# A hybrid attention and convolution block on one core: raw compressed values computed in channel layout

## The chip, the cores and the metric

The kernel runs on one NeuronCore of one Trainium2 chip. The metric is device time in microseconds (us) of one execution. TensorE (PE) multiplies, VectorE (DVE) and ScalarE (ACT) work on tiles and read and write PSUM, GpSimd (POOL) works on SBUF tiles, and the SP queue issues most DMAs. PEld is the weight load of TensorE, which runs beside its matmuls.

## The reference

One decoder block on x of shape (1, 512, 1024), float32:

- h = rms_norm(x), then one wide product h @ w_in, which is split into queries, three pairs of keys and values (compressed, selected, window; 4 groups of 64 channels each), attention gates, two convolution inputs and two merge gates.
- Compressed keys and values: `compress_blocks` cuts the 512 tokens of a group into blocks of 32 with a stride of 16, adds a position embedding, flattens a block to 32 x 64 numbers, and runs `silu(blocks @ w1) @ w2`. Keys are rotated (rope) ahead of it, values are not.
- Attention: 16 heads in 4 groups, three softmax branches (compressed, selected, window), summed with gates.
- A causal convolution of 31 taps over 1024 channels, layer norm over the channels, silu, and a product with w_conv_out; merged with the attention by two gates, multiplied by w_out and added to x.
- A SwiGLU feed-forward part with 2816 hidden channels, and a final rms_norm.

## The kernel before

Every float32 product is made of three matmuls with operands split into a high and a low part (`mm3`, lines 211 to 213). A weight piece is loaded raw by SP (`wr`, line 120), rounded by ACT to its high part (`wh`, line 136), and POOL (DVE in some stages) subtracts to get the low part (`wl`, line 137).

A product with w_in comes in two layouts. **Token layout** (`tok_g`): the activations hT are the stationary operand, 256 columns of weights move, and a PSUM tile `ptk` holds 2 x 128 tokens by 256 channels; 256 output channels take 96 matmuls of 256 columns. **Channel layout** (`chan_g`): a weight block is the stationary operand, all 512 tokens move, and a PSUM tile `pch` holds 128 channels by 512 tokens; 256 output channels take 48 matmuls of 512 columns. Both take their two PSUM tiles from the pool `dense`, two buffers.

The work around the change stands in this program order: convolution inputs (`ub_g`, `ua_g`), then `cmp_raw(C_KC, True)` for raw compressed keys, `cmp_raw(C_VC, False)` for raw compressed values, `keys(C_KS, 0)`, `cmp_prep` and `keys(C_KW, 1)`, then `cmp_mlp` for the compressed keys beside the selected values, and so on up to the first queries. `cmp_raw` fills two chunk buffers `kcraw` of 128 x 512: rows 0 to 63 hold the even tokens of two groups, rows 64 to 127 the odd ones. Its inner function `evT` (line 449) makes each buffer with four ACT copies of 64 x 256 from a PSUM tile that holds channels by tokens. In `cmp_raw` for values the token layout is used, ACT copies each `ptk` to SBUF (`kd`, line 458), and TensorE transposes it back to channels by tokens in eight 128 x 128 transposes (`tv`, line 466).

`cmp_prep` later adds the positions on DVE (`kctmp`, line 488), rounds on ACT (`kchi`, line 491) and subtracts on DVE (`kclo`, line 492). `cmp_mlp` multiplies them (`phid`). The convolution's 31 taps per channel block are DVE instructions on a PSUM accumulator (`cacc`, line 794) that lie between all of this.

Attention runs as 32 units (4 groups, 2 head pairs, 4 query blocks). A unit makes its scores in PSUM tiles `sc` (lines 700 to 703, pool of two buffers), DVE takes the maxima (`nm`, line 705), ACT the exponentials (`P`, line 708), DVE makes the factors `R` (lines 715 and 718), ACT scales P with them (line 723), TensorE transposes P (`tP`, line 732), ACT and DVE split that (`pth`, `ptl`, lines 735 and 736), and TensorE multiplies with the values (`pv`, lines 756 to 760), from where ACT copies to `pvt` (line 763). Products with w_in and w_conv_out in small steps are put between these (`fill`). The layer norm of the convolution is done in five stages between units 16 and 21: among them `pstat` and `pvar` (matmuls on lines 811 and 826), eight subtractions of the mean on DVE (line 815), eight multiplications on DVE (line 833), and eight Silu on ACT (line 835), which need another activation table than the exponentials.

The order on each engine is not the program order. The framework's scheduler lists the instructions by its own estimate of when each may run, and each engine then runs its list in order. An edit early in the program can therefore move instructions far behind it.

Of the kernel before, what the change touches and what calls it, by code (L numbers as in the profile page):

```python
# [10 lines left out]
F32 = mybir.dt.float32  # L11
# [11 lines left out]
NT = S // 128  # L23
# [13 lines left out]
def hybrid_block(  # L37
# [8 lines left out]
    nc = tc.nc  # L46
# [15 lines left out]
    pa = astack.enter_context(tc.tile_pool(name="att", bufs=1))  # L62

    def acts(name, dt=F32):
        return ap.tile([128, S], dt, name=name, tag="A")
# [16 lines left out]
    def trp(name):  # L82
        return ps.tile([128, 512], F32, name=name, tag="tr", bufs=2)


    idn = cp.tile([128, 128], F32, name="idn")
# [80 lines left out]
    hT_hi = [acts(f"hThi{k}", F32R) for k in range(KT)]  # L167
    hT_lo = [acts(f"hTlo{k}", F32R) for k in range(KT)]
# [15 lines left out]
    for th in range(2):  # L184
# [6 lines left out]
        for k in range(KT):  # L191
            p = trp("hT")
            for j in range(2):
                nc.tensor.transpose(p[:, j * 128:(j + 1) * 128], hs[2 * th + j][:, k * 128:(k + 1) * 128], idn)
            ev = nc.scalar.activation(hT_hi[k][:, hsl], p[:, :256], AF.Copy, scale=g_mix[:, k:k + 1])  # L195
# [19 lines left out]
    def chan_g(src, c0, act_hi, act_lo, evac, ncol=256, halves=((0, S),), ws=None):  # L215

        nm_ = (ncol + 127) // 128
        given, ws = ws, ws or []

        def part(p, m, kh, kk, n0=0, n1=S):  # L220
            wh, wl = ws[kh][kk]
            w = min(128, ncol - 128 * m)
            sl = slice(128 * m, 128 * m + w)
            k = 4 * kh + kk
            mm3(p[:w, n0:n1], wh[:, sl], wl[:, sl], act_hi[k][:, n0:n1], act_lo[k][:, n0:n1],
                k == 0, k == KT - 1)

        fine = phase["fine"]
        if fine:
            ws.append(wload(src, 0, 4, c0, ncol))  # L230
            yield 0
        p = [dense("pch") for _ in range(nm_)]
        for n0, n1 in halves:
            for kh in range(2):
                if not fine and not given and n0 == 0:
                    ws.append(wload(src, 4 * kh, 4, c0, ncol))
                for m in range(nm_):
                    if fine and m == 0 and kh == 0:
                        ws.append(wload(src, 4, 4, c0, ncol))
                    for kk in range(4):  # L240
                        part(p[m], m, kh, kk, n0, n1)
                        if fine and kk < 3:
                            yield 640
                    if kh and n1 == S:
                        evac(m, p[m])
                    if fine:
                        yield 640
                if not fine:
                    yield 0

    def tok_g(src, c0, act_hi, act_lo, evac, tts=(0, 1, 2, 3)):

        nu = len(tts) // 2
        ws = []

        def part(p, u, kh, j, kk):
            wh, wl = ws[kh][kk]
            t = tts[2 * u + j]
            sl = slice(128 * t, 128 * t + 128)
            k = 4 * kh + kk  # L260
            mm3(p[:, 256 * j:256 * j + 256], act_hi[k][:, sl], act_lo[k][:, sl], wh, wl,
                k == 0 and j == 0, k == KT - 1)

        fine = phase["fine"]
        if fine:
            ws.append(wload(src, 0, 4, c0, 256))
            yield 0
        p = [dense("ptk") for _ in range(nu)]
        for kh in range(2):
            if not fine:  # L270
                ws.append(wload(src, 4 * kh, 4, c0, 256))
            elif kh == 0:
                ws.append(wload(src, 4, 4, c0, 256))
            for u in range(nu):
                for j in range(2):
                    for kk in range(4):
                        part(p[u], u, kh, j, kk)
                        if fine and kk % 2 and (kk, j) != (3, 1):
                            yield 640
                if kh:  # L280
                    evac(tts[2 * u], p[u].rearrange("p (j c) -> p j c", j=2))
                if fine:
                    yield 640
            if not fine:
                yield 0

    def chan(*a, **k):
        for _ in chan_g(*a, **k):
            pass

    def tok(*a, **k):
        for _ in tok_g(*a, **k):
            pass
# [26 lines left out]
    for bits in (7, 15, 24, None):  # L320
        if bits is None:
            part = rest
        else:
            q = 2.0 ** (bits - 3)
# [44 lines left out]
    def run_all(*gens):  # L369
        gens = list(gens)  # L370
        while gens:
            for g_ in list(gens):
                if next(g_, gens) is gens:
                    gens.remove(g_)
# [44 lines left out]
    def roped_tokens(c0, evT):  # L419

        tiles = []

        def ev(u, p):
            kd = pa.tile([128, 2, 4, 64], F32, name="kd", tag="pt", bufs=5)
            nc.scalar.copy(kd[:, :, :, 16:64], p.rearrange("p j (h d) -> p j h d", d=64)[:, :, :, 16:64])

            def dst(A, B):
                nc.vector.tensor_add(kd[:, :, :, 0:16], A, B)

            rope_rows(p, u, 4, dst)  # L430
            tiles.append(kd)

        yield from tok_g(w_in, c0, hT_hi, hT_lo, ev)
        for gp in range(2):
            q = trp("tk")
            for t in range(NT):
                src = tiles[t // 2][:, t % 2, 2 * gp:2 * gp + 2, :].rearrange("p g d -> p (g d)")
                nc.tensor.transpose(q[:, 128 * t:128 * t + 128], src, idn)
            evT(gp, q)


    def cmp_raw(c0, roped):
        raw = [pa.tile([128, S], F32, name="kcraw", tag="q", bufs=8) for _ in range(2)]

        def evT(gp, q):
            for gg in range(2):
                v = q[64 * gg:64 * gg + 64, :].rearrange("p (u a) -> p a u", a=2)
                for a in range(2):
                    nc.scalar.copy(raw[gp][64 * a:64 * a + 64, 256 * gg:256 * gg + 256], v[:, a, :])

        if roped:
            run_all(roped_tokens(c0, evT))
            return raw
        tiles = []

        def ev(u, p):
            kd = pa.tile([128, 2, 4, 64], F32, name="kd", tag="pt", bufs=5)
            nc.scalar.copy(kd.rearrange("p j h d -> p j (h d)"), p)
            tiles.append(kd)

        tok(w_in, c0, hT_hi, hT_lo, ev)
        for gp in range(2):
            q = trp("tv")
            for t in range(NT):
                src = tiles[t // 2][:, t % 2, 2 * gp:2 * gp + 2, :].rearrange("p g d -> p (g d)")
                nc.tensor.transpose(q[:, 128 * t:128 * t + 128], src, idn)
            evT(gp, q)
        return raw

    def cmp_prep(raw, pos, w2):  # L470
# [167 lines left out]
    def query_split(qd, pr):  # L638
# [11 lines left out]
        return res  # L650

    raw_k = cmp_raw(C_KC, True)
    raw_v = cmp_raw(C_VC, False)
    vals = []
    run_all(keys(C_KS, 0))
# [298 lines left out]
    for n in range(32):  # L954
        g, pr, i = n // 8, n // 4 % 2, n % 4
# [166 lines left out]
    for t in range(NT):  # L1122
        sl = slice(128 * t, 128 * t + 128)

        for c in ((0, 256), (256, 512)) if t == NT - 1 else ((0, 512),):
# [3 lines left out]
            j = 1 + c[0] // 256  # L1129
# [40 lines left out]
```

## Time and profile before

| | us |
|---|---|
| median of three runs | 975.17 (974.79 to 975.36) |
| the profiled execution's own time | 974.84 |
| its span, first to last instruction | 973.1 |
| TensorE busy in the span | 940.4 |
| VectorE, ScalarE, GpSimd busy | 633.1, 545.1, 234.9 |

The span is cut by stage as follows: norm and convolution inputs up to about 85 us, keys, values and compression up to about 200 us, attention with the convolution's end up to about 530 us, w_out and the feed-forward part to the end. In lines of the timeline the columns are start, duration, engine, line, operation, output <- inputs, tile shape, count, and in square brackets the idle time of the engine before and what ended it. Matmul durations in them overlap; what one costs in a stream is the distance between starts.

### The profile page before, as it was taken

To read this page: it belongs to the slowest core of one execution; us is meant where nothing else is said; L and a number is where in the kernel's file an instruction comes from. 1 tells how busy PE (TensorE), PEld (TensorE's weight loads), DVE (VectorE), ACT (ScalarE), POOL (GpSimd) and SP (SyncE) were. 2 spreads that over 40 slices of the span, in tenths; PEclk is the share of its full clock that TensorE was granted. 3 is DMA by queue.
4 is the path that set the end of the run, shared out by engine and by line. 5 is a ranking of instruction groups with operands and counts; after the bars stand their busy time and mean duration, and the time that the engine had idled before them with its cause. 6 is when DMAs were issued, how large, how long until landed. Compare 5 with 4: busy or idle time off the path is not lost.

```text
span 973.1 us, 14959 instructions
## 1 busy us (share of the span) xinstructions
PE 940.4 (97%) x5306; PEld 797.5 (82%) x5306; DVE 633.1 (65%) x1254; ACT 545.1 (56%) x1273; POOL 234.9 (24%) x256
## 2 busy tenths in 40 slices
PE   5999989899999999989999999999999999999996
PEld 5889979888888977877778878988888888888886
DVE  6799999987999987676876877633333343322512
ACT  6533545558879887999984776533333333322412
POOL 3545447853353342622322000000000000000000
PEclk9999989999999999999999999999999999999999
DMA  7333324542121111111212166633333323322302
GB/s 225 90 106 88 87 72 121 134 109 55 45 66 44 34 45 44 44 33 55 98 56 76 59 201 188 180 96 100 91 105 88 107 87 108 97 96 95 118 29 87
DMA packets 77599, 89.03 MB, mean 91 GB/s; under 512 B 5896, under 2 KB 65620, under 8 KB 77524
## 3 DMA queue, kind: packets, MB, share of 16 engines
q1 hardware_dynamic: 76676, 87.38, 30.0%
q8 instruction: 42, 0.69, 0.3%
q0 software_dynamic: 144, 0.52, 0.2%
q14 instruction: 33, 0.27, 0.1%
q10 hardware_dynamic: 704, 0.17, 0.1%
HBM read 85.96 MB, written 2.10 MB: 90 GB/s over the span
## 4 chain that ended last, share of the span: by engine, by line
PE 85%; DVE 7%; ACT 4%; issue 1%; DMA 1%; POOL 1%; SPq 0%; POOLq 0%; ACTq 0%; DVEq 0%
PE pf L211 8%; PE pf L212 8%; PE pf L213 8%; PE pch L213 7%; PE pch L211 7%; PE pch L212 7%; PE ptk L211 4%; PE ptk L212 4%; PE ptk L213 4%; PE pd L211 4%; PE pd L213 4%; PE pd L212 4%; PE tP L732 3%; PE sc L700 2%; PE sc L701 2%; PE pv L756 2%
## 5 line engine op out<-in xcount | busy, mean ns | idle before, releaser
L137 POOL TENSOR_TENSOR wl<-wr,wh 128x512 fp32r<-128x512 f32 x128 | 167.2, 1318 | 229.8 <-ACT wh L136 179.5
L136 ACT CAST wh<-wr 128x512 fp32r<-128x512 f32 x228 | 140.1, 622 | 145.0 <-PE pf L212 52.6
L794 DVE SCALAR_TENSOR_TENSOR cacc<-z,cw,cacc 128x512 f32<-128x512 f32 x232 | 165.5, 748 | 3.8 <-ACT cacc L792 1.7
L211 PE MATMUL pf<-h2hi,wh 128*128 128x512 f32 (+1 forms) x384 | 142.3, 372 | 0.6 <-ACT h2hi L1034 0.6
L212 PE MATMUL pf<-h2lo,wh 128*128 128x512 f32 (+1 forms) x384 | 142.5, 372 | 0.0
L213 PE MATMUL pf<-h2hi,wl 128*128 128x512 f32 (+1 forms) x384 | 142.4, 372 | 0.0
L137 DVE TENSOR_TENSOR wl<-wr,wh 128x512 fp32r<-128x512 f32 x100 | 68.7, 689 | 109.6 <-ACT wh L136 108.1
L213 PE MATMUL pch<-hThi,wl 128*128 128x512 f32 (+1 forms) x272 | 107.3, 395 | 1.5 <-POOL wl L137 1.5
L211 PE MATMUL pch<-hThi,wh 128*128 128x512 f32 (+1 forms) x272 | 107.3, 396 | 1.2 <-ACT hThi L195 1.2
L212 PE MATMUL pch<-hTlo,wh 128*128 128x512 f32 (+1 forms) x272 | 107.5, 396 | 0.0
L149 DVE TENSOR_TENSOR wl<-wr,wh 128x512 fp32r<-128x512 f32 x76 | 51.6, 689 | 61.9 <-ACT wh L148 61.8
L148 ACT CAST wh<-wr 128x512 fp32r<-128x512 f32 (+1 forms) x84 | 50.1, 604 | 73.7 <-PE pd L213 50.9
L708 ACT ACTIVATE P<-sc,nm 128x32 f32<-128x32 f32 (+3 forms) x192 | 84.7, 446 | 11.2 <-DVE nm L705 9.2
L1136 POOL TENSOR_TENSOR rstd<-rstd,half 128x1 f32<-128x1 f32 x4 | 2.2, 547 | 359.6 <-DVE rstd L1135 359.6
L211 PEld LDWEIGHTS pf<-h2hi,wh 128*128 128x128 f32 x384 | 72.0, 188 | 13.2 <-ACT h2hi L1034 0.8
L211 PE MATMUL ptk<-wh,hThi 128*128 128x256 f32 x288 | 82.7, 287 | 0.0
L213 PEld LDWEIGHTS pf<-h2hi,wl 128*128 128x128 f32 x384 | 72.2, 188 | 12.6
L212 PEld LDWEIGHTS pf<-h2lo,wh 128*128 128x128 f32 x384 | 72.2, 188 | 12.4
L212 PE MATMUL ptk<-wl,hThi 128*128 128x256 f32 x288 | 81.2, 282 | 0.0
L213 PE MATMUL ptk<-wh,hTlo 128*128 128x256 f32 x288 | 81.0, 281 | 0.0
L705 DVE TENSOR_REDUCE nm<-sc 128x1 f32<-128x32 f32 (+3 forms) x192 | 68.8, 381 | 16.8 <-PE sc L703 15.5
L211 PE MATMUL pd<-wh,ahi 128*128 128x512 f32 (+1 forms) x184 | 70.0, 380 | 0.8 <-DVE x L1092 0.8
(234 smaller groups left out, 2133.0 us busy)
## 6 DMA issues: line engine op xcount, KB each, us to landing
wr<-in_w_in_dram SPq DMA_DIRECT2D x100, 256.0 KB, 2.8
wr<-in_w_ffn_gate_dram SPq DMA_DIRECT2D x48, 256.0 KB, 2.7
wr<-in_w_ffn_up_dram SPq DMA_DIRECT2D x48, 256.0 KB, 2.7
wr<-in_w_ffn_down_dram SPq DMA_DIRECT2D x44, 256.0 KB, 2.5
wr<-in_w_out_dram SPq DMA_DIRECT2D x32, 256.0 KB, 2.6
x<-in_x_dram SPq DMA_DIRECT2D x8, 512.0 KB, 5.0
wr<-in_w_conv_out_dram SPq DMA_DIRECT2D x16, 256.0 KB, 2.7
wr<-in_cmp_k_w_dram SPq DMA_DIRECT2D x8, 256.0 KB, 2.6
```

The lines of the kernel that those rows point to most:

```text
L136: nc.scalar.copy(hi[:, sl, :ncol], raw[:, sl, :ncol])
L137: eng.tensor_sub(lo[:, sl, :ncol], raw[:, sl, :ncol], hi[:, sl, :ncol].bitcast(F32))
L148: nc.scalar.copy(hi, raw)
L149: (nc.vector if phase["lo_dve"] else nc.gpsimd).tensor_sub(lo, raw, hi.bitcast(F32))
L211: nc.tensor.matmul(o, lh, rh, start=first, stop=False, skip_group_check=True)
L212: nc.tensor.matmul(o, lh, rl, start=False, stop=False, skip_group_check=True)
L213: nc.tensor.matmul(o, ll, rh, start=False, stop=last, skip_group_check=True)
L700: nc.tensor.matmul(sc[:, :e - a], qh[:, tsl], K[:, a:e], start=True, stop=False)
L705: nc.vector.tensor_reduce(out=nm[:, b:b + 1], in_=sc[:, ba - a:be - a], axis=AX.X, op=OP.max, negate=True)
L708: nc.scalar.activation(P[:, ba:be], sc[:, ba - a:be - a], AF.Exp, bias=nm[:, b:b + 1], accum_out=Dn[:, b, hh:hh + 1])
L732: nc.tensor.transpose(t4[:, 256 * b + 128 * hh:256 * b + 128 * hh + 128], Ps[hh][:, key_blk(j, b)], idn)
L794: nc.vector.scalar_tensor_tensor(cts[c] if j == TAPS - 1 else a, z[:, j:j + S], cw[:, j, c:c + 1], a, op0=OP.mult, op1=OP.add)
```

## The change

In `cmp_raw` the raw values are now made with the channel layout, and `evT` copies each finished PSUM tile straight into its chunk buffer. The SBUF tiles `kd` of the values, their two ACT copies and the eight transposes are gone. All lines below move up by 13.

```diff
@@ cmp_raw
         if roped:
             run_all(roped_tokens(c0, evT))
             return raw
-        tiles = []
-
-        def ev(u, p):
-            kd = pa.tile([128, 2, 4, 64], F32, name="kd", tag="pt", bufs=5)
-            nc.scalar.copy(kd.rearrange("p j h d -> p j (h d)"), p)
-            tiles.append(kd)
-
-        tok(w_in, c0, hT_hi, hT_lo, ev)
-        for gp in range(2):
-            q = trp("tv")
-            for t in range(NT):
-                src = tiles[t // 2][:, t % 2, 2 * gp:2 * gp + 2, :].rearrange("p g d -> p (g d)")
-                nc.tensor.transpose(q[:, 128 * t:128 * t + 128], src, idn)
-            evT(gp, q)
+        chan(w_in, c0, hT_hi, hT_lo, evT)
         return raw
```

The lists of the engines differ from there on. Three places follow, each before and after.

**ACT at the raw values.** Before, the copies of the transposed raw keys are followed by casts of weights (`wh`), the two copies to `kd`, and eight copies to the chunk buffers from `tv`:

```order
L449 COPY kcraw<-tk 64x256 x8
L136 CAST wh<-wr 128x512 x2
L458 COPY kd<-ptk 128x512
L136 CAST wh<-wr 128x512
L458 COPY kd<-ptk 128x512
L136 CAST wh<-wr 128x512
L449 COPY kcraw<-tv 64x256 x8
```

After:

```order
L449 COPY kcraw<-tk 64x256 x8
L136 CAST wh<-wr 128x512 x2
L449 COPY kcraw<-pch 64x256 x4
L136 CAST wh<-wr 128x512 x2
L449 COPY kcraw<-pch 64x256 x4
```

The two copies to `kd` are gone, and the eight chunk copies now come in two fours, one behind each `pch`.

**DVE at the preparation of the compressed keys** (`kst` is the low part of the selected keys, `kctmp` and `kclo` belong to the compressed ones). Before:

```order
L488 TENSOR_TENSOR kctmp<-kcraw,cpos 128x8x64
L566 TENSOR_TENSOR kst_837<-tk,kst_837 64x128
L488 TENSOR_TENSOR kctmp<-kcraw,cpos 128x8x64
L566 TENSOR_TENSOR kst_837<-tk,kst_837 64x128
L488 TENSOR_TENSOR kctmp<-kcraw,cpos 128x8x64 x2
L492 TENSOR_TENSOR kclo<-kctmp,kchi 128x8x128
L566 TENSOR_TENSOR kst_837<-tk,kst_837 64x128
L492 TENSOR_TENSOR kclo<-kctmp,kchi 128x8x128
```

After (line 488 is now 475, 566 is 553, 492 is 479):

```order
L475 TENSOR_TENSOR kctmp<-kcraw,cpos 128x8x64
L553 TENSOR_TENSOR kst_837<-tk,kst_837 64x128
L475 TENSOR_TENSOR kctmp<-kcraw,cpos 128x8x64 x2
L553 TENSOR_TENSOR kst_837<-tk,kst_837 64x128
L475 TENSOR_TENSOR kctmp<-kcraw,cpos 128x8x64
L553 TENSOR_TENSOR kst_837<-tk,kst_837 64x128
L479 TENSOR_TENSOR kclo<-kctmp,kchi 128x8x128 x2
```

Three subtractions for `kst` instead of two now stand between the first `kctmp` and the first `kclo`.

**ACT at the last stage of the convolution's norm**, beside units 21 and 22 of the attention. Before, from the copy `pvt` to the table load of the exponentials (`ct` are the convolution's channel blocks):

```order
L763 COPY pvt<-pv 64x256
L835 ACT_TABLE_LOAD
L835 ACTIVATE ct_2182<-ct_2182,vec 128x512
L723 ACTIVATE P<-P,R 128x256 x4
L835 ACTIVATE ct_2184<-ct_2184,vec 128x512
L835 ACTIVATE ct_2379<-ct_2379,vec 128x512
L835 ACTIVATE ct_2381<-ct_2381,vec 128x512
L835 ACTIVATE ct_2461<-ct_2461,vec 128x512
L835 ACTIVATE ct_2956<-ct_2956,vec 128x512
L835 ACTIVATE ct_3567<-ct_3567,vec 128x512
L835 ACTIVATE ct_4007<-ct_4007,vec 128x512
L708 ACT_TABLE_LOAD
```

After (723 is now 710, 835 is 822), the first five of these rows; seven more Silu and the table load of the exponentials follow:

```order
L750 COPY pvt<-pv 64x256
L136 CAST wh<-wr 128x512
L710 ACTIVATE P<-P,R 128x256 x4
L822 ACT_TABLE_LOAD
L822 ACTIVATE ct_2120<-ct_2120,vec 128x512
```

A cast and all four scalings of P now stand ahead of the table load, and all eight Silu behind it. On PE, between the product with the compressed values (`pv<-pc`) and the first score matmul of unit 22 that waits for these exponentials, there stand 33 `pch` matmuls of 512 columns and eight transposes before, 17 and eight after; the rows just ahead of that score matmul are, after:

```order
L211 MATMUL pch<-hThi_127,wh 128x512
L212 MATMUL pch<-hTlo_135,wh 128x512
L213 MATMUL pch<-hThi_127,wl 128x512
L211 MATMUL pch<-hThi_128,wh 128x512
L212 MATMUL pch<-hTlo_136,wh 128x512
L213 MATMUL pch<-hThi_128,wl 128x512
L687 MATMUL sc<-kst_836,qhi 128x416
```

The 16 `pch` matmuls that are missing there stand behind it now.

## Rows read from the trace of the kernel before

**Rows 1.** The page: busy time, share of the span and instructions of each engine.

```profile
PE 940.4 (97%) x5306; PEld 797.5 (82%) x5306; DVE 633.1 (65%) x1254; ACT 545.1 (56%) x1273; POOL 234.9 (24%) x256
```

**Rows 2.** PE's waits in the whole run: total us, times, longest.

```profile
PE sc L700 <- ACT P L708: 3.1, 2, 2.9
PE phid L213 <- DVE kclo L492: 2.4, 1, 2.4
PE pv L757 <- DVE ptl L736: 2.3, 2, 1.9
...
PE phid L211 <- ACT gate L605: 1.4, 1, 1.4
```

**Rows 3.** Timeline of PE at the raw keys and values, 83 to 110 us.

```profile
83.64 0.39 PE L211 MATMUL pch<-hThi,wh 128*128 128x512 f32 x1
...
85.01 0.28 PE L211 MATMUL ptk<-wh,hThi 128*128 128x256 f32 x1
...
95.92 0.60 PE L438 MATMUL tk<-idn,kd 128*128 128x128 f32 x4
...
108.12 0.60 PE L466 MATMUL tv<-idn,kd 128*128 128x128 f32 x4
...
108.97 0.65 PE L466 MATMUL tv<-idn,kd 128*128 128x128 f32 x4
...
109.58 0.28 PE L211 MATMUL ptk<-wh,hThi 128*128 128x256 f32 x1
```

**Rows 4.** Timeline of ACT: the chunk copies of the raw keys.

```profile
99.47 3.02 ACT L449 COPY kcraw<-tk 64x256 f32<-64x256 f32 x8 [2.35 <-PE tk L438]
```

**Rows 5.** Timeline of DVE from the raw values to the compressed keys.

```profile
98.80 18.52 DVE L794 SCALAR_TENSOR_TENSOR cacc<-z,cw,cacc 128x512 f32<-128x512 f32 x28
118.12 0.29 DVE L407 TENSOR_TENSOR ropeA<-ptk,cos 128x128 f32<-128x128 f32 x1 [0.80 <-ACT kd L425]
...
139.16 1.22 DVE L492 TENSOR_TENSOR kclo<-kctmp,kchi 128x1024 fp32r<-128x1024 f32 x1
140.40 0.29 DVE L566 TENSOR_TENSOR kst<-tk,kst 64x128 fp32r<-64x128 f32 x1
```

**Rows 6.** A window: length, busy us of five engines, PE's granted clock, DMA share, GB/s.

```profile
440.00:442.00 2.00, 2.00 (x9) 1.59 (x9) 0.96 (x4) 1.49 (x7) 0.00 (x0) 0.50 0.00 0
```

**Rows 7.** Timeline of PE at units 21 and 22 of the attention.

```profile
426.11 0.28 PE L760 MATMUL pv<-pc,vcmp 128*128 128x256 f32 x1
...
434.59 0.39 PE L213 MATMUL pch<-hThi,wl 128*128 128x512 f32 x1
437.85 0.46 PE L700 MATMUL sc<-kst,qhi 128*128 128x416 f32 x1 [2.87 <-ACT P L708]
```

**Rows 8.** Timeline of ACT over the same stretch.

```profile
425.15 1.12 ACT L136 CAST wh<-wr 128x512 fp32r<-128x512 f32 x2
426.48 0.37 ACT L763 COPY pvt<-pv 64x256 f32<-64x256 f32 x1 [0.20 <-PE pv L760]
426.87 1.28 ACT L835 ACT_TABLE_LOAD   x1
...
428.89 1.71 ACT L723 ACTIVATE P<-P,R 128x256 f32<-128x256 f32 x4
430.50 5.05 ACT L835 ACTIVATE ct<-ct,vec 128x512 f32<-128x512 f32 x7
435.56 1.28 ACT L708 ACT_TABLE_LOAD   x1
436.86 0.58 ACT L708 ACTIVATE P<-sc,nm 128x384 f32<-128x384 f32 x1
```

**Rows 9.** Timeline of POOL and DVE: the factors R beside POOL's weight work, and later.

```profile
425.83 3.00 POOL L137 TENSOR_TENSOR wl<-wr,wh 128x512 fp32r<-128x512 f32 x2 [6.60 <-ACT wh L136]
...
427.60 1.26 DVE L718 TENSOR_TENSOR R<-R,gate 128x6 f32<-128x6 f32 x1
...
442.82 0.17 DVE L718 TENSOR_TENSOR R<-R,gate 128x6 f32<-128x6 f32 x1
```

## The prediction

> **What bounds the kernel now.** I read the page's busy line first: TensorE is busy for 940.4 of 973.1 us [rows 1], so some 33 us are not TensorE work, and a change counts by the TensorE work it takes away and by the waits of TensorE that it makes or removes. The second view is the list of PE's waits [rows 2]. The reader is to see how few there are: one of 2.4 us on DVE at the compressed keys (`phid` on `kclo`), one of 1.4 us on ACT (`phid` on the gates), one of 1.9 us on DVE and one of 2.9 us on ACT in the attention. Nearly everywhere else matmuls follow each other, so there is little to win by a better order and much to lose by a worse one. Third, the timelines of PE, DVE and ACT at the three places where the lists of the engines differ [rows 3, 5, 7, 8].
>
> **The change part by part.** I sum against the profiled execution (974.84; its span of 973.1 and 1.7 around it) and add 0.33 at the end, since the median is 975.17.
>
> *The product itself.* In token layout 96 matmuls of 256 columns ran from 85.01 to 95.92, 0.1136 each; six `pch` matmuls of 512 columns ran from 83.64 to 85.01, 0.2283 each [rows 3]. So 96 x 0.1136 = 10.91 becomes 48 x 0.2283 = 10.96: a loss of 0.05. The layout alone buys nothing, since a column costs the same in both.
>
> *The eight transposes.* From the first `tv` at 108.12 to the matmul at 109.58 there are 1.46 us [rows 3], in which three more `ptk` matmuls run (3 x 0.1136 = 0.34). So the transposes cost 1.12, all of it on PE, which does not wait here. Together with the layout the sum is 1.06 saved.
>
> *ACT's copies.* Two copies of 128 x 512 to `kd` go away and eight chunk copies stay, in fours. The copies now hold the PSUM tiles of `dense`, but a group of four takes 1.5 (eight of this shape took 3.02 [rows 4]), and the next product into that tile starts one half product later (12 x 0.2283 = 2.7). ACT, busy for 56% of the span [rows 1], puts two casts for weights of a later half product behind each four. So they lie beside PE's work and I take nothing; if a tile came free late after all, it would cost the 1.5 of one group less the 2.7 of cover, which is still nothing.
>
> *DVE up to the compressed keys.* DVE is full of taps here, 0.66 each (28 in 18.52), but it waited 0.80 for ACT and PE ahead of the rope of the next keys [rows 5]. So it follows PE, and it comes to `kctmp` 1.06 earlier as PE does; two taps that leave this stretch only lengthen that wait. Then one more subtraction `kst` stands ahead of the first `kclo`, for which PE waits 2.4 [rows 2]: 0.29 [rows 5] plus a gap, 0.33. Of the 1.06, 0.73 is left behind this place; if that subtraction finds a gap, all of it.
>
> *The gates.* PE waited 1.4 ahead of the `phid` of the compressed values for a gate copy [rows 2]. In the new lists one tap more (0.66) stands on DVE and one cast more (0.56, half of 1.12 [rows 8]) on ACT ahead of that copy, and four `ptk` matmuls (0.46) are pulled in front of the waiting `phid`. So between 0.46 gained and 0.66 + 0.56 - 0.46 = 0.76 lost; I take 0.3 lost, nearer to the loss, since DVE goes from tap to tap in all of this stage.
>
> *The mean of the convolution.* Between `pstat` and the `pv` matmul that waited 1.9 for DVE behind eight subtractions [rows 2], there were 7 matmuls of 512 columns and 29 of 256 besides the scores and transposes, now 11 and 17: 4.89 becomes 4.44. What DVE has to do in between is the same, so the wait grows by 0.45 (bounds 0 and 0.45).
>
> *The Silu block.* This is the largest term. Before, ACT copies `pvt` at 426.48, loads a table, does one Silu, four scalings of P, seven Silu, loads the other table, and at 436.86 makes the exponentials that free the score tile; PE's score matmul then starts at 437.85 [rows 7, 8]. That chain is 11.37 long. PE has 33 matmuls of 512 columns and eight transposes to do beside it, is through at 434.9 and waits 2.87. In the new lists the chain is 0.37 (`pvt`) + 0.56 (cast) + 1.61 (scalings, 428.89 to 430.50) + 1.28 + 8 x 0.72 (seven take 5.05) + 1.28 + 0.99 (436.86 to 437.85) = 11.86, 0.49 more. The scalings need R, which DVE had at 428.86; in the old list a table load and one Silu filled the time until then, in the new one ACT stands still from 427.41 on, up to 1.45. Behind the waiting scalings are queued all eight Silu and every exponential of unit 22, and PE waits for those. And PE has 16 matmuls less to fill the time, 16 x 0.2283 = 3.65. The wait grows by 3.65 + 0.49 = 4.1 if R is early and by 5.6 if it is as late as before. Early or late is set by POOL: R's small multiplication took 1.26 and ended at 428.86, with POOL's two weight subtractions that ended at 428.83, and a later one of the same shape took 0.17 [rows 9]. The new list has four casts around this point instead of two, so four subtractions on POOL, and I take 5.4.
>
> The Trainium skill (GPSIMD Engine Reference, section Specifications) says that POOL shares its SBUF interfaces with VectorE and that instructions with two SBUF inputs contend. By that rule the four subtractions make R late and the term is 5.4 or more; were the two engines free of each other, it would be 4.1. The trace agrees with the rule by its 1.26 against 0.17.
>
> *The clock.* A long wait also halves the granted clock: 0.50, the lower of its two levels, in the whole window of 440 to 442 behind the wait of 2.87 [rows 6, 7]. A slow window of 2 us loses 1.0. A wait of 8 us may lengthen the slow stretch by up to one such window, or change nothing where ACT is last anyway; I take 0.4.
>
> The sum: 974.84 - 1.06 + 0.33 + 0.3 + 0.45 + 5.4 + 0.4 = 980.7, and 0.33 for the median gives **981.0**. The lower ends of all terms add to 977.4 and the upper ones to 981.9, with the 0.33 to 977.8 and 982.3: the range of this case.
>
> **The rivals.**
>
> *Only the saving arrives.* If ACT were well ahead of PE at the Silu block, or the exponentials of unit 22 were done before it, the missing 16 matmuls would cost nothing. Then 974.84 - 1.06 + 0.33 + 0.33 = 974.4; with the gates and the mean at their upper ends, 975.7. Against it: ACT waited 0.20 for PE's `pv` at 426.48 [rows 8], so it cannot run ahead, and it works its list in order. For it: the list could leave a gap elsewhere that I count as unchanged. It decides where ACT has its exponentials done before the Silu begin, that is some 7 us ahead of PE. Chance 0.16.
>
> *Weight loads.* If the weight loads and not the columns set the pitch of the pairs, 48 pairs less would free 48 x 0.1136 = 5.5, and with the Silu term the time would be 975.5. Against it stands that a column costs the same in both layouts here [rows 3]. The Trainium skill (TensorE: Matmul & The Clock Gate, back-to-back issue gap) gives 131 ns for a sustained 512-column matmul with its weight load; by it this product would take 6.3 and the kernel would gain 4.6 more. The rows have 228 ns, and so it gets little chance: 0.05.
>
> *More waits behind the Silu (slower still).* In unit 23, three score tiles are used again after some 1.6 us of PE work, counted from the lists with the pitches above, where there were 2.1 to 3.5. The exponentials that free a tile take 0.99 [rows 7, 8], a maximum on DVE comes ahead of them, and behind the Silu ACT has work piled up (`gt`, casts of 0.56). If ACT is still behind when unit 23 comes, each of the three tiles waits for one to two such casts or copies, 0.5 to 1.2, together 1.5 to 3.6: 982.5 to 984.6. It decides from the point at which ACT's pile is longer than the matmuls between two uses of a tile. Chance 0.12.
>
> *Something falls into place.* A wait of rows 2 may vanish by a lucky order: below 973.2, chance 0.05.
>
> **How the numbers follow.** My case has the remaining 0.62. A measurement of this kernel can tell about 0.2%, or 1.95 us, from no change: 973.2 to 977.1 is no change. That takes the saving alone and the weight loads, 0.21; faster is 0.05, and slower is 0.62 + 0.12 = 0.74. The range leaves out what is below 974.2 and above 983.6.
>
> **What would show it.** In the trace of the changed kernel: no `tv` and no ACT copy from `ptk` to `kd` of 128 x 512, 48 `pch` matmuls 0.228 apart in their place, and the selected keys' matmuls some 1.1 us earlier. PE's wait for `kclo` some 0.3 longer. ACT's scalings ahead of the table load, eight Silu in one piece, and one PE wait on ACT P at a score matmul of 7 to 8.5 us (were the scalings early, 7), with the clock at half behind it. Wrong would be: that wait still near 3; a time under 977; or TensorE's busy time falling by much more than 1 us.

## The result, and the profile after

The changed kernel takes 987.34 us (median; 986.15 to 988.13) where the kernel before takes 974.98 beside it: a ratio of 1.0127, with a 95% interval of 1.0111 to 1.0143, or 12.4 us slower. The forecast was 981.0 with a range up to 983.6. The direction was right, and the time lies outside the range.

TensorE has less to do and the span is longer. The page's busy line of the changed kernel, answering to [rows 1]:

```profile
PE 944.5 (96%) x5250; PEld 796.4 (81%) x5250; DVE 635.5 (64%) x1254; ACT 546.1 (55%) x1271; POOL 237.2 (24%) x256
```

56 matmuls are gone, and yet PE's busy time is 4.1 us higher: part of the matmuls ran at the lower clock (the mean granted clock is 0.987 in this execution and 0.992 in that of [rows 1]). PE's waits (total us, times, longest), answering to [rows 2]; lines are now 13 lower:

```profile
PE sc L687 <- ACT P L695: 7.2, 2, 7.1
PE pv L744 <- DVE ptl L723: 3.6, 5, 1.8
PE phid L213 <- DVE kclo L479: 2.2, 1, 2.2
PE tP L719 <- ACT P L710: 2.1, 4, 1.0
PE phid L211 <- ACT kchi L478: 2.1, 1, 2.1
PE ptk L211 <- ACT wh L136: 1.7, 1, 1.7
...
PE ptk L212 <- POOL wl L137: 1.0, 1, 1.0
PE tPc L729 <- DVE P L712: 0.9, 1, 0.9
```

The wait on the exponentials grew from 2.9 to 7.1. The gates' wait of 1.4 became 1.7 and 1.0, at other matmuls (`ptk`). Several small waits (`tP`, `tPc`, `pv`) are new.

**The raw values** did what the change says. PE's timeline: the first of the last 37 `pch` matmuls, and the first matmul behind them. ACT's: the first four chunk copies.

```profile
99.67 0.47 PE L213 MATMUL pch<-hThi,wl 128*128 128x512 f32 x1
...
108.23 0.28 PE L211 MATMUL ptk<-wh,hThi 128*128 128x256 f32 x1
```

```profile
105.68 1.50 ACT L449 COPY kcraw<-pch 64x256 f32<-64x256 f32 x4 [1.75 <-PE pch L213]
```

37 matmuls in 8.56 us are 0.231 each, the transposes are gone, and PE waits nowhere for the copies.

**The gates.** PE's timeline, where [rows 2] had one wait of 1.4, and a window behind it (length, busy us of five engines, granted clock, DMA share, GB/s):

```profile
173.34 0.38 PE L211 MATMUL ptk<-wh,hThi 128*128 128x256 f32 x1 [1.73 <-ACT wh L136]
174.69 0.39 PE L212 MATMUL ptk<-wl,hThi 128*128 128x256 f32 x1 [0.97 <-POOL wl L137]
```

```profile
176.00:178.00 2.00, 2.00 (x9) 1.67 (x9) 2.00 (x4) 0.54 (x2) 2.00 (x2) 0.50 0.71 231
```

The granted clock fell to its lower level (0.50) behind these two waits. It had stayed at 1.00 behind the single wait of 1.4.

The first wait is for a cast of weights. On ACT that cast stands behind a gate copy, and the gate copy waits for DVE's second split (`v`). ACT in the changed kernel:

```profile
172.29 0.21 ACT L592 ACTIVATE gate<-pvg 128x48 f32<-128x48 f32 x1 [1.30 <-DVE v L564]
...
172.65 1.67 ACT L136 CAST wh<-wr 128x512 fp32r<-128x512 f32 x3
```

PE's `thid`, the last rows that it does in both kernels ahead of these waits, and DVE's first two splits. Before, then after:

```profile
171.68 0.38 PE L518 MATMUL thid<-idn,hid 128*128 128x128 f32 x2
```

```profile
169.98 0.42 DVE L577 TENSOR_TENSOR v<-pvg,v 128x256 fp32r<-128x256 f32 x1
170.31 0.74 DVE L794 SCALAR_TENSOR_TENSOR cacc<-z,cw,cacc 128x512 f32<-128x512 f32 x1
170.97 0.41 DVE L577 TENSOR_TENSOR v<-pvg,v 128x256 fp32r<-128x256 f32 x1
```

```profile
171.22 0.38 PE L505 MATMUL thid<-idn,hid 128*128 128x128 f32 x2
```

```profile
170.06 0.42 DVE L564 TENSOR_TENSOR v<-pvg,v 128x256 fp32r<-128x256 f32 x1
170.40 1.54 DVE L781 SCALAR_TENSOR_TENSOR cacc<-z,cw,cacc 128x512 f32<-128x512 f32 x2
171.84 0.42 DVE L564 TENSOR_TENSOR v<-pvg,v 128x256 fp32r<-128x256 f32 x1
```

Against `thid` the first split starts 1.70 ahead before and 1.16 ahead after, the second 0.71 ahead before and 0.62 behind after. So DVE's second split is 1.33 later against PE: 0.54 of that is made ahead of the gates, and 0.79 by one tap more between the two splits. PE's waits here grew by about as much, by 1.30.

**The Silu block**, answering to [rows 7, 8]. PE, then ACT, then POOL and DVE:

```profile
435.25 0.44 PE L719 MATMUL tP<-idn,P 128*128 128x128 f32 x2 [0.97 <-ACT P L710]
...
438.32 0.39 PE L213 MATMUL pch<-hThi,wl 128*128 128x512 f32 x1
445.77 0.72 PE L687 MATMUL sc<-kst,qhi 128*128 128x416 f32 x1 [7.06 <-ACT P L695]
```

```profile
434.68 1.71 ACT L710 ACTIVATE P<-P,R 128x256 f32<-128x256 f32 x4 [1.03 <-DVE R L705]
436.41 1.28 ACT L822 ACT_TABLE_LOAD   x1
437.71 5.75 ACT L822 ACTIVATE ct<-ct,vec 128x512 f32<-128x512 f32 x8
...
444.77 0.58 ACT L695 ACTIVATE P<-sc,nm 128x384 f32<-128x384 f32 x1
```

```profile
431.64 6.14 POOL L137 TENSOR_TENSOR wl<-wr,wh 128x512 fp32r<-128x512 f32 x4 [4.13 <-ACT wh L136]
```

```profile
433.41 1.24 DVE L705 TENSOR_TENSOR R<-R,gate 128x6 f32<-128x6 f32 x1
```

ACT waits 1.03 for R, which DVE makes in 1.24 beside POOL's four subtractions; then come the scalings, the table and eight Silu in one piece. PE is out of work at 438.7 and waits 7.06. Behind it the clock is low until about 452. The last of those windows:

```profile
450.00:452.00 2.00, 2.00 (x8) 1.28 (x7) 0.56 (x1) 1.32 (x4) 1.36 (x2) 0.50 0.33 109
```

The rows show where PE stands, and not which part of the change made it stand there. The theory: the layout is innocent and gains its 1.06, and the whole loss is the new order. The rival: the layout itself costs (its PSUM tiles, its copies). A third: a new order is bad only at the Silu block.

### The profile page after: what moved, and what is told of

Same layout as the page of the kernel before. It is cut to its first block, busy times and chain, and to the rows that moved or that the text cites. A ratio compares the mean times of both kernels' runs of the same rounds, so it can differ in the third digit from the quotient of the medians.

```text
span 986.4 us, 14856 instructions
## 1 busy us (share of the span) xinstructions
PE 944.5 (96%) x5250; PEld 796.4 (81%) x5250; DVE 635.5 (64%) x1254; ACT 546.1 (55%) x1271; POOL 237.2 (24%) x256
## 4 chain that ended last, share of the span: by engine, by line
PE 81%; DVE 7%; ACT 6%; issue 3%; POOL 2%; DMA 1%; SPq 0%; POOLq 0%; ACTq 0%; DVEq 0%
PE pf L212 8%; PE pf L211 8%; PE pf L213 8%; PE pch L212 6%; PE pch L211 6%; PE pch L213 6%; PE pd L211 4%; PE pd L212 4%; PE pd L213 4%; PE ptk L213 4%; PE ptk L212 4%; PE ptk L211 4%; PE tP L719 3%; PE sc L687 2%; PE pv L744 2%
## 5 line engine op out<-in xcount | busy, mean ns | idle before, releaser
L212 PE MATMUL pch<-hTlo,wh 128*128 128x512 f32 (+1 forms) x288 | 114.2, 397 | 0.0
L211 PE MATMUL pch<-hThi,wh 128*128 128x512 f32 (+1 forms) x288 | 113.2, 395 | 1.0 <-ACT hThi L195 1.0
L213 PE MATMUL pch<-hThi,wl 128*128 128x512 f32 (+1 forms) x288 | 112.5, 391 | 1.5 <-POOL wl L137 1.5
L211 PE MATMUL ptk<-wh,hThi 128*128 128x256 f32 x256 | 73.8, 288 | 1.7 <-ACT wh L136 1.7
L212 PE MATMUL ptk<-wl,hThi 128*128 128x256 f32 x256 | 72.7, 284 | 1.0 <-POOL wl L137 1.0
L213 PE MATMUL ptk<-wh,hTlo 128*128 128x256 f32 x256 | 72.8, 284 | 0.0
```

What stands on the lines that cost most here:

```text
L211: nc.tensor.matmul(o, lh, rh, start=first, stop=False, skip_group_check=True)
L212: nc.tensor.matmul(o, lh, rl, start=False, stop=False, skip_group_check=True)
L213: nc.tensor.matmul(o, ll, rh, start=False, stop=last, skip_group_check=True)
```

## The experiments

Kernels that ran together share their runs of the kernel before, whose median was 974.88 with e1 to e4, 971.54 with e5 to e8 and 975.10 with e9 to e12. So ratios are compared, and 0.001 is about 1 us. Their 95% intervals are 0.001 to 0.002 to either side. Profiles are single executions.

Most of the kernels pin the order: one function at the end of the trace chains each engine's instructions in the order of a table, without making any of them wait for another's end.

```diff
+def pin(nc, tc):
...
+    for e, steps in lists.items():
+        row = [by[e][n] for n in itertools.accumulate(steps)]
+        for a, b in zip(row, row[1:]):
+            tc.add_manual_dep(b, a.name, how, reason="list")
```

**e1: the new layout with the old lists.** The changed kernel with the function above and the table of the kernel before. At the raw values every second slot of the 96 matmuls is kept, and the copies to `kcraw` stand, in fours, where those to `kd` stood.

> The changed kernel, with every engine's instructions pinned to the order that they had in the kernel before; only at the raw values do 48 matmuls stand for 96 and the transposes and two copies fall out. If the loss comes from the new lists alone, the layout's saving of 1.06 is left: 974.98 - 1.06 = 973.9 us (973.0 to 975.0). If the channel layout itself costs (its PSUM tiles held by chunk copies, the weights' order), the time stays above 984. If the old lists only fitted the old moments, and an early stage that ends 1.1 us sooner breaks the fit, between 975 and 980.

973.8 us, ratio 0.9989 (0.998 to 0.9998): faster by 1.1 (0.2 to 2.0), as the layout was to give. In the traces its engines' lists differ from those of the kernel before only at the raw values. PE's waits are those of [rows 2] again:

```profile
PE sc L687 <- ACT P L695: 3.7, 3, 2.9
...
PE phid L211 <- ACT gate L592: 1.4, 1, 1.4
```

**e2: the old layout with the new lists.** The kernel before, transposes and all, with the table of the changed kernel.

> The kernel before, layout and transposes kept, with every engine pinned to the order that it has in the changed kernel. If the lists alone make the loss, the time is the changed kernel's plus the 1.06 that the transposes cost: 988.4 us (987.4 to 989.4). If the layout makes it, 975. If both do a part, in between, and the part of each is read off.

988.16 us, ratio 1.0137 (1.0123 to 1.0151), 0.0010 or 1.0 us above the changed kernel, which two intervals of this size do not set apart from nothing. Its lists differ from the changed kernel's only at the raw values. With either list the new layout is no slower than the old one, so the 13.5 us between e1 and the changed kernel are the list's. The rival falls.

The next runs give the changed kernel the old lists in one stretch at a time. The stretches were cut where both lists have done the same instructions.

**e3: the gates, as first cut.** In effect only PE's order changed there:

```diff
 L505 MATMUL thid<-idn,hid 128x128 x2
-L211 MATMUL ptk<-wh,hThi_121 128x256
-L212 MATMUL ptk<-wl,hThi_121 128x256
-L213 MATMUL ptk<-wh,hTlo_129 128x256
-L211 MATMUL ptk<-wh,hThi_122 128x256
 L211 MATMUL phid<-wh,kchi 128x256
```

> The changed kernel with its own lists everywhere, but for the stretch of the gates (about 165 to 195 us), where every engine has the order of the kernel before. There the trace of the changed kernel has waits of 1.73 and 0.97 us instead of one of 1.40, and the granted clock falls to 0.50 behind them, which it did not do before. If these are real losses that add to the end, 987.34 - 1.3 - 1.5 = 984.5 us (983.8 to 985.3). If a later wait takes them back, 987.3.

988.04 us, ratio 1.0136 (1.0121 to 1.0152): nothing gained. The expectation said every engine, but the cut on ACT and DVE lay behind the gates, so the run tells only that PE's order there is not the cause. PE waited 2.9 in one piece for the gate copy, where it had waited 1.73 and 0.97.

**e4: the Silu block and all behind it.** The old table from about 405 us on. On ACT:

```diff
 L822 ACT_TABLE_LOAD
 L822 ACTIVATE ct_2120<-ct_2120,vec 128x512
+L710 ACTIVATE P<-P,R 128x256 x4
 L822 ACTIVATE ct_2122<-ct_2122,vec 128x512
```

> The changed kernel with its own lists up to about 405 us and the lists of the kernel before from there on (the norm of the convolution with its Silu block and all that follows). If the prediction's Silu term is right, PE's longest wait for the exponentials shrinks from 7.06 to about 3, the 0.97 at the transposes of P goes, and the slow stretch of the clock is shorter by some 1.5: 987.34 - 5.1 - 1.5 = 980.7 us (979.5 to 982.2). If waits in units 23 and later follow the Silu in any order, over 983.

982.28 us, ratio 1.0071 (1.0058 to 1.0084): 0.0056 or 5.5 us less. PE's waits on the exponentials:

```profile
PE sc L687 <- ACT P L695: 3.8, 3, 2.9
```

From there on, the loss is real and about as large as forecast. It is also less than half of the loss, which the third theory did not allow.

**e5: the gates on every engine.** The old table from 169 to 200 us. On DVE:

```diff
-L781 SCALAR_TENSOR_TENSOR cacc<-z,cw,cacc 128x512 x3
+L781 SCALAR_TENSOR_TENSOR cacc<-z,cw,cacc 128x512 x5
 L564 TENSOR_TENSOR v_1696<-pvg,v_1696 128x4x64
-L781 SCALAR_TENSOR_TENSOR cacc<-z,cw,cacc 128x512 x2
+L781 SCALAR_TENSOR_TENSOR cacc<-z,cw,cacc 128x512
 L564 TENSOR_TENSOR v_1696<-pvg,v_1696 128x4x64
```

> The changed kernel with the order of the kernel before between about 169 and 200 us on every engine, its own order elsewhere. (In e3 the stretch was cut too late on ACT and DVE, whose own order at the gates stayed, and PE waited 2.9 us there all the same.) If the gates' loss lies in the order of DVE's and ACT's rows there, PE's wait is back at 1.4, the granted clock does not fall behind it, and of 987.3 some 2.8 to 3.5 us go: 984.2 us (983.5 to 985.0). If a later wait takes it back, or the wait was made ahead of 169 us, 987.

984.01 us, ratio 1.0124 (1.0109 to 1.0139): again nothing. (The time is the one that I expected, but only since the kernel before took 971.54 beside it.) PE's timeline there, and DVE's first split (`v`):

```profile
170.22 0.38 PE L505 MATMUL thid<-idn,hid 128*128 128x128 f32 x2
...
174.13 0.58 PE L211 MATMUL phid<-wh,kchi 128*128 128x256 f32 x1 [3.53 <-ACT gate L592]
```

```profile
170.64 0.42 DVE L564 TENSOR_TENSOR v<-pvg,v 128x256 fp32r<-128x256 f32 x1
```

The wait is 3.53, with the order of the kernel before, where it was 1.40. What differs is when the engines arrive: DVE's first split starts 0.42 behind PE's `thid`, where it starts 1.16 ahead in the changed kernel and 1.70 ahead in the kernel before. Part of this is the run's own making. The changed kernel does two taps fewer ahead of the second keys, and where the old table begins, at 169 us, these two still have to be done: they are the two that the rows above put ahead of the split. So e5 shows that the old order at the gates alone brings nothing back, and not that the order there costs nothing.

**e10: the second keys, the compressed keys and the gates.** The old table from 110 to 200 us. On DVE, the first of the changes:

```diff
-L781 SCALAR_TENSOR_TENSOR cacc<-z,cw,cacc 128x512 x26
+L781 SCALAR_TENSOR_TENSOR cacc<-z,cw,cacc 128x512 x28
 L407 TENSOR_TENSOR ropeA<-ptk,cos_445 128x128
```

> The changed kernel with the order of the kernel before from about 110 to 200 us (second keys, compressed keys, gates) on every engine, its own order elsewhere. In e5 the old order of the gates alone left the wait at 3.5 us: DVE came to the gates' splits at the same time in all lists, and PE came sooner. Theory: DVE's order in the keys' stage (two taps fewer ahead of the rope of the second keys, so that DVE stands 1.2 us for PE, and the same work is done 1.1 to 1.4 later) sets that. Then the wait is back at 1.4, the clock stays up, and 1.0127 becomes 1.0085 to 1.0095 (some 3.5 us less). If it is the number of matmuls ahead of the gates alone, 1.012.

984.05 us, ratio 1.0094 (1.0073 to 1.0115): 3.2 us less than the changed kernel, with some 2.6 to either side. The same rows as for e5:

```profile
170.39 0.38 PE L505 MATMUL thid<-idn,hid 128*128 128x128 f32 x2
172.17 0.39 PE L211 MATMUL phid<-wh,kchi 128*128 128x256 f32 x1 [1.40 <-ACT gate L592]
```

```profile
168.68 0.42 DVE L564 TENSOR_TENSOR v<-pvg,v 128x256 fp32r<-128x256 f32 x1
```

DVE is 1.71 ahead of PE again, the wait is 1.40, and the clock stays at 1.00 behind it. So the gates' loss lies in the order from 110 to 200 us, of the keys' stage and the gates together. The splits above put 0.54 of the later DVE down to the stage ahead of the gates. Two rows show part of that. First the four `kclo` of the changed kernel, then those of e10 (duration min/median/max in ns, first and last start):

```profile
L479 DVE TENSOR_TENSOR kclo<-kctmp,kchi x4: 1216/1470/1807, 138.8 to 166.2; 128x1024 fp32r<-128x1024 f32 x4
```

```profile
L479 DVE TENSOR_TENSOR kclo<-kctmp,kchi x4: 1207/1221/1839, 138.6 to 164.5; 128x1024 fp32r<-128x1024 f32 x4
```

Three of the four take the same in both. The last takes 1.72 in the changed kernel (from 166.19) and 1.21 in e10 (from 164.53). POOL subtracts weights beside it from its start to its end in both, so POOL's presence alone does not explain it. DVE also stands longer for the second keys, where [rows 5] had 0.80:

```profile
117.42 0.29 DVE L407 TENSOR_TENSOR ropeA<-ptk,cos 128x128 f32<-128x128 f32 x1 [1.15 <-ACT kd L425]
```

No run has the old order in the keys' stage alone, so how much of the 3.2 each of the two stages costs is not shown.

**e6: the units of the attention.** The old table from 200 to 407 us. PE's list differs over all of that stretch; its first rows:

```diff
 L212 MATMUL pch<-hTlo_130,wh 128x512
-L213 MATMUL pch<-hThi_122,wl 128x512
 L687 MATMUL sc<-kst_834,qhi 128x288
-L211 MATMUL pch<-hThi_123,wh 128x512
 L505 MATMUL thid<-idn,hid 128x128 x2
```

> The changed kernel with the order of the kernel before between about 200 and 407 us (the units of the attention up to the convolution's mean), its own order elsewhere. The trace of the changed kernel has some twenty small waits of PE there (tP, tPc, pv, sc; 0.1 to 1.0 each) that the old order does not have, and falls back by about 4.6 us beyond the old pace. If these are the order's: 987.3 - 4.6 = 982.7 us (981.7 to 984). If they come from where the stretch begins and not from its order, 986 or more.

979.5 us, ratio 1.0076 (1.0063 to 1.0089): 5.0 us less. PE's waits between 205 and 400 us, the changed kernel first and e6 second:

```profile
PE pv L744 <- DVE ptl L723: 3.2, 4, 1.8
PE tPc L729 <- DVE P L712: 0.9, 1, 0.9
PE tP L719 <- ACT P L710: 0.7, 2, 0.5
...
```

```profile
PE pv L744 <- DVE ptl L723: 1.9, 1, 1.9
...
```

In this window the waits fall from 5.3 to 2.1; in the changed kernel none is over 1 us but the old one of 1.8. Near the end of its stretch e6 has one that neither the kernel before nor the changed one has:

```profile
402.31 0.28 PE L687 MATMUL sc<-kst,qhi 128*128 128x32 f32 x1 [1.12 <-ACT P L695]
```

So over the whole stretch the waits fall by 2.0, and 3.0 of the 5.0 are not settled. The changed kernel's profiled execution has a stretch at the lower clock behind the wait of 1.8, and e6's has none, but this stretch comes and goes on one and the same list (last section).

The parts add up: 3.2 + 5.0 + 5.5 = 13.7 against 13.5 between e1 and the changed kernel. Each part is known to 2 or 3 us only, so that they meet so closely is in part luck.

**e7: another small edit at the same place.** The kernel before with two dead transposes, listed freely.

```diff
                 nc.tensor.transpose(q[:, 128 * t:128 * t + 128], src, idn)
+            nc.tensor.transpose(q[:, 384:512], src, idn)
             evT(gp, q)
```

> The kernel before with two transposes more at the raw values (each group's last one is done twice, into the same place), listed by the scheduler. Their own price is 2 x 0.14 = 0.28 us (eight took 1.12). Theory: any small edit there makes the scheduler list a large part of the kernel anew (1848 places of PE differ), and a new list has more waits than the old one: 978 to 988 us. Rival: the changed kernel's list is an unlucky one and most new lists are as good as the old: 974.5 to 976.

981.22 us, ratio 1.0098 (1.0081 to 1.0116). Its waits have the Silu block of the changed kernel (lines one higher than before):

```profile
PE sc L701 <- ACT P L709: 7.1, 1, 7.1
```

At the gates it waits only 1.1. From about 384 us on, the rows of PE, DVE and ACT in its trace are those of the changed kernel, one for one by line, tile and shape. So it is a second new list up to there, and the same one behind.

**e12: the same two transposes in the old order.** e7 with the function and the old table, the two transposes behind the last one of their group.

> The kernel of e7 (the kernel before with two transposes more) with every engine pinned to the order of the kernel before, the two standing behind the last transpose of their group. If e7's 9.7 us were the new list's and not the transposes', what is left is their own price, 2 x 0.14 = 0.28 us: ratio 1.0003, between 0.9995 and 1.001. If two more transposes at that place hold something up, 1.005 or more.

976.36 us, ratio 1.0012 (1.0002 to 1.0022). The two transposes cost 1.2 us (0.2 to 2.1), more than I expected, with the 0.28 of the estimate still inside the interval. The other 8.4 of e7's 9.6, to about 2, are its list. So two different edits, one that removes work and one that adds some, both fell out of an order that fitted better. Since their lists are one behind 384 us, whether most orders are worse than the old one is not shown.

**e8 and e9: the Silu block taken apart.** The new layout with the old table up to unit 21. The Silu is made of a tanh, which is in the table of the exponentials (e8's trace has no table load behind 420 us), and two DVE instructions. The halves of `lng` and `lnb` are taken ahead of it.

```diff
-                nc.scalar.activation(cc[c], cc[c], AF.Silu, scale=lng[:, c:c + 1], bias=lnb[:, c:c + 1])
+                nc.scalar.activation(t, cc[c], AF.Tanh, scale=lng[:, c:c + 1], bias=lnb[:, c:c + 1])
+                nc.vector.tensor_scalar(cc[c], cc[c], lng[:, c:c + 1], lnb[:, c:c + 1], op0=OP.mult, op1=OP.add)
+                nc.vector.scalar_tensor_tensor(cc[c], t, 1.0, cc[c], op0=OP.add, op1=OP.mult)
```

In e8 they come in threes, behind eight multiplications in one piece.

> The changed kernel with the order of the kernel before up to unit 21, and the last stage of the convolution's norm made without the Silu: a tanh, which needs no other table than the exponentials, and two DVE instructions per channel block, in threes after units 21, 22 and 23; from there on the scheduler lists freely. If the Silu block (two table loads, eight Silu in one piece) is what makes PE wait 2.87 us and the clock fall behind it, then 973.8 - 2.9 - 1.0 = 969.9 us (969 to 971). If the free list behind it brings new waits, or the 17 more DVE instructions do, 972 to 980.

973.6 us, ratio 1.0019 (1.0006 to 1.0032). Not the 969.9 that I expected: that wait on ACT is gone and one on DVE has come, behind the pile.

```profile
438.80 0.58 PE L744 MATMUL pv<-ptl,v 128*128 128x256 f32 x1 [4.37 <-DVE ptl L723]
```

In e9 one channel block comes between two steps of the units.

```diff
+            if n == 21:
+                taps = silu_steps()
+            else:
+                conv_norm(stages.index(n))
```

> As e8, but the multiplication by the norm, the tanh and the two DVE instructions of one channel block are put between two steps of units 22 and 23, block by block, where e8 had eight multiplications and three blocks in one piece ahead of DVE's ptl, for which PE waited 4.4 us. If that pile on DVE was what took the Silu's gain away, no wait of PE over 1.5 is left behind 400 us, and the kernel is at 0.9945 to 0.9965 of the one before (970 us where that takes 975). If DVE cannot take the work between its splits at all, waits of 0.5 to 1 follow in units 22 and 23, and it stays at 0.9989 (as e1) or above.

972.7 us, ratio 0.9976 (0.9964 to 0.9988): faster than both kernels by its interval, and less than I expected. From e1 (0.9989) the intervals do not set it apart, so that the tanh gains on the Silu is not shown. Behind 400 us one wait on DVE over 1 us is left:

```profile
439.75 0.39 PE L747 MATMUL pv<-pc,vcmp 128*128 128x256 f32 x1 [2.64 <-DVE pc L733]
```

**e11: the tanh steps in a free list.** The changed kernel with e9's code and no table.

> The changed kernel with the norm's last stage made by tanh block by block as in e9, and no order pinned anywhere: the scheduler lists all of it. If the Silu block is what the new list handles worst, its wait of 7.06, the 0.97 ahead of it and the slow clock behind it go in this list too: 1.0127 less 0.0075 to 0.0085, that is 1.004 to 1.0055 (979 to 980.3 us where the kernel before takes 975). If the wait moves to DVE's splits, 1.008 or more.

985.27 us, ratio 1.0107 (1.009 to 1.0125), a miss. The wait of 7.06 is gone, and between 410 and 530 us PE waits for many small things instead:

```profile
PE pv L743 <- ACT pth L722: 0.9, 1, 0.9
PE pv L744 <- DVE ptl L723: 0.7, 1, 0.7
```

The slow clock did not go, though the expectation had it go. From 440 to 446 us it is at 0.50, as in this window:

```profile
442.00:444.00 2.00, 2.00 (x5) 1.57 (x6) 2.00 (x5) 2.00 (x5) 0.54 (x1) 0.50 0.02 4
```

The waits are much shorter than the one they replace, and the profiled execution gained 5.5 (a span of 980.9 against 986.4). But it was the fastest of its six runs, by 2.6 us under their median, and the changed kernel's was the slowest of its four. So this profile does not stand for the medians, and why these differ by only 2 us is open.

## Why the prediction was wrong

Set against the stretches: for the keys and gates 0.6 was forecast and e10 measures 3.2, for the units 0.45 and e6 measures 5.0, for the Silu block with its clock 5.8 and e4 measures 5.5. So the direction and the largest term were right, and the loss that was missed is in the first two.

- **The product and the transposes: right.** -1.06 was forecast; e1 gives -1.1 (-0.2 to -2.0), and the changed kernel against e2 -1.0, to about 2.
- **ACT's copies: right.** Fours of 1.50, and no wait of PE behind them.
- **The compressed keys: not to be told.** +0.33 was forecast for `kclo`. That wait went from 2.4 to 2.2, and the one on `kchi` ahead of it, which [rows 2] leaves out, from 1.5 to 2.1, together +0.4. But with the same list up to there, the two together are 3.9 in e3, 4.5 in e4 and 3.8 in e5, so a difference of 0.4 can't be told from single profiles.
- **The gates: the step that failed first.** +0.3 was forecast, with 0.76 as the upper end. e10 measures 3.2 for the keys and gates. Three things were wrong in it. I counted rows from the last common point on, as if DVE came to that point at the same distance from PE as before, and had written that the two taps that leave the keys' stage only lengthen a wait of DVE; it came 0.54 later. The tap more that I did count, at 0.66, cost 0.79, and the four `ptk` matmuls that I took as 0.46 of cover waited for their own weights (1.73 and 0.97): the waits grew by 1.30, past my upper end. And the clock fell behind waits that I had priced at their own length.
- **The mean of the convolution: wrong, and small.** +0.45 was forecast; the wait is 1.8 where it was 1.9. (In e5's profile, with the same list there, no such wait is seen.)
- **The Silu block: right.** +5.4 was forecast; the two waits of 0.97 and 7.06 less 2.87 are 5.2. R came late, as assumed: 1.24 beside POOL. That this goes with POOL rests on more than the one pair of rows in the prediction: in both profiles, of the 32 multiplications of this line none that ran clear of POOL took over 0.17, and beside POOL's subtractions they took up to 1.26. The Trainium skill (GPSIMD Engine Reference, section Specifications) has VectorE and GpSimd share SBUF interfaces and contend where a VectorE instruction has two SBUF inputs. These rows agree with it; the `kclo` rows of e10 do not decide on it.
- **The clock: too small.** 0.4 was forecast for one place. Behind the Silu the clock is low up to 452, and behind the gates it fell where it had not before. Counted from the windows at half pace, that is up to 1.5 more behind the Silu and up to 1.7 behind the gates, an estimate from single executions.
- **The units between 200 and 407 us: the term that was missing.** The sum held nothing for them but the 0.45 of the mean, and e6 measures 5.0. I read the lists at the places where the kernel before already waited, and took all other differences, at more than a thousand places on PE, as free. The few waits of [rows 2] were read as a property of the kernel. e1, e2, e7 and e12 show that they are a property of one list: both new lists have waits at places where the old one has none, and so they cannot be found by looking at the old waits. That the units' order costs is shown; 2.0 of the 5.0 are waits, and what the rest is stays open.

The rival that the channel layout frees weight loads fell as well: 0.231 for a 512-column matmul, and e1 gains no more than the transposes. "More waits behind the Silu" did not come as described either: behind the wait of 7.06, up to 560 us, PE has one wait over 0.15, of 0.44 at 519.55, and e4 shows the loss from the Silu block on at 5.5, the size of the term itself.

## What to carry to other kernels

Where a scheduler lists the instructions and one engine is busy for 97% of the span, an edit can cost far more through the list that it produces than it saves: here 1 us of saved work stood against 13.5 us of new order. Read the difference of the lists over the whole program, not at the old waits; where two engines run close behind each other, ask how far apart they arrive. If the old order is good, pin it and change only what the edit needs: that turned a loss of 12.4 us into a gain of 1.1.

## What was not expected of the hardware

The same wait is not always followed by a lower clock. The wait of 1.87 on `ptl` stands in the profiled executions of the kernel before and of e1, with the same list. The windows behind it, before first and e1 second:

```profile
392.00:394.00 2.00, 2.00 (x10) 1.75 (x9) 0.40 (x2) 1.98 (x9) 1.19 (x1) 0.50 0.00 0
```

```profile
392.00:394.00 2.00, 2.00 (x16) 1.59 (x15) 1.06 (x3) 1.98 (x8) 1.85 (x2) 1.00 0.00 0
```

At 0.50 PE began 10 matmuls in these 2 us, at 1.00 it began 16. Of the four profiles with this wait and the list of the kernel before, those of the kernel before and of e12 have the low clock, those of e1 and e9 (1.77 there) do not. Between the same two matmuls around it (from 194.63 to 409.60 before, from 195.36 to 409.26 in e1) the first took 214.97 us and the second 213.90, so the low clock cost some 1.1 here. So what a wait of this length costs differs from one execution to the next, and the clock's share of a loss of a few microseconds can't be told from one profile.
